# A decoder block on one core: the order of VectorE's work in a Strassen step, and five steps more in Strassen form

## The chip, the core and the metric

The kernel runs on one core of a Trainium2 chip. The metric is the device time of one execution in microseconds, as the median of several runs. The engines are TensorE (PE in the profile, its weight loads PEld), VectorE (DVE), ScalarE (ACT), GpSimd (POOL) and SyncE (SP); transfers run on queues that SP and POOL feed.

## What is computed

The block normalizes a 256x4096 activation, multiplies it with one wide projection, mixes one part by causal averages over four window lengths and one by a gated short convolution, multiplies both with branch weights, merges them by sigmoid gates, multiplies with an output matrix, adds the input, and normalizes again. Cut to what matters:

```
h = rmsnorm(x, norm_w[l])
proj = jnp.einsum('bsd,de->bse', h, w_in[l])              # 4096 x 20480
u_p, z_p, u_c, b_c, c_c, z_c, g_logit = jnp.split(proj, SPLIT_POINTS, axis=-1)
y_pool = causal_multiscale_pool(u_p, pool_w[l], pool_scale[l]) * jax.nn.silu(z_p)
y_conv = causal_gated_shortconv(u_c, b_c, c_c, conv_w[l], conv_b[l]) * jax.nn.silu(z_c)
br = jnp.einsum('bsnc,ncd->bsnd', jnp.stack([y_pool, y_conv], axis=2), w_branch[l])   # 2 x 2048 x 4096
merged = jnp.sum(jax.nn.sigmoid(g_logit.reshape(b, s, 2, d) + gate_b[l]) * br, axis=2)
x = x + jnp.einsum('bsd,de->bse', merged, w_out[l])       # 4096 x 4096
return rmsnorm(x, final_norm_w)
```

All is float32. The kernel writes each factor as a high part, rounded to the format that TensorE multiplies, and a low part, the rest. A product is three matmuls: high by high, high by low, low by high.

## The kernel before

**Units and steps.** The work is a list of units, each 1024 output columns for all 256 rows. In order: cu0, cc0, cz0, cb0 and the same four with 1 (convolution branch), pz0, pu0, pz1, pu1 (pooling branch), eight gate units g0_0, g1_0, g0_1 to g1_3, eight branch units b0_0, b1_0 to b1_3 and four output units o0 to o3. A unit runs over its inner dimension in steps of 256 rows of weights: 16 steps, in a branch unit 8. `SEQUENCES` (L627) has one letter for each step. `p` is a plain step: 2 halves of columns, 2 of inner rows, 2 of tokens and 3 matmuls of 128x512, so 24 matmuls. `s` and `u` are steps in Strassen form: seven products of halves, each of 3 matmuls, so 21. `b` and `m` in two units are the pooling's own matmuls. The rows of cu0 and of the last branch unit, b1_3, are all plain; b0 and b1 stand for all other branch units.

**Preparing a step.** A step's 1 MB of weights lands in one of three `raw` buffers, asked for on SP's queue as soon as the step three places before is split (`pump`, L1199). Then `micros` (L278) writes its high and low parts into pages of `ring`, 16 pages of a 128x512 pair each. For a plain step that is twice: ScalarE rounds 128x1024 (`split_act`, L257), VectorE subtracts (`split_sub`, L261); 4 pages. A Strassen step needs four sums of weight quarters beside three quarters as they are, 7 pages:

- `sums`: VectorE adds the first quarter to the second and third, 128x1024 into `V`. In a *helped* step this isn't done by VectorE: the quarters are loaded into a free corner of `E` or `R` and POOL's queue adds the others on the way. A step with `s` is helped if a corner is free in time; a step with `u` never is.
- `direct`: ScalarE rounds three quarters (128x1536); VectorE adds the third sum into the first quarter of `raw`, subtracts for the three quarters, and adds the fourth sum into the second quarter.
- `t13`: high and low of the first two sums.
- `t24`: high and low of the third and fourth sum, one 128x1024 on ScalarE and one on VectorE.

A page is free again when TensorE has used it, and ScalarE, the first to write, waits for that. Every engine works in the order in which the program issues (`keep_in_program_order`). Steps are prepared up to three (AHEAD) before TensorE's own.

**Multiplying.** A Strassen step's products go to eight banks of sums: four that plain steps use too (`sums`, PE[t][n]), and four more (`shared`). In code: `order = N3, M1, M2, N7, N5, N6, N4`, where N3, M1, M2 use the pages of `direct`, N7, N5 those of `t13`, N6, N4 those of `t24`. The first six matmuls go to a `sums` bank and a shared one, and the tenth, the first of N7, to `shared(2)`. In a unit that ends with a Strassen step that step's order is N3, M2, N4, M1, N7, N5, N6.

**Around a unit's end.** The shared banks are joined by `joins` (L450): on VectorE four to six operations of 128x512 from them into `R`. If the unit's last Strassen step is not its last step, the joins are queued early, one for every six matmuls of the step that follows; else `combine` (L497) issues them behind the last step. Then `R` and `E` are added, and a unit's own epilogue follows by such ticks: for cb0 (`b_epi`, L675) a load of `E`, a multiplication of `R` by `E`, and 16 transposes of `R` on TensorE through the shared banks, whose results VectorE multiplies into `Y`.

Of the kernel before, what the change touches and what calls it, by code (L numbers as in the profile page):

```python
# [59 lines left out]
def hybrid_block(ctx: ExitStack, tc: tile.TileContext, x, x_t, norm_t, w_first, w_in, pool_w, pool_scale,  # L60
# [10 lines left out]
    def act(dst, src, func=AF.Copy, **kw):  # L71
        return pin(nc.scalar.activation(dst, src, func, **kw))  # L72

    def tt(dst, a, b, op):
        return pin(nc.vector.tensor_tensor(out=dst, in0=a, in1=b, op=op))  # L75
# [4 lines left out]
    def add(dst, a, b):  # L80
        return tt(dst, a, b, ALU.add)

    def sub(dst, a, b):
        return tt(dst, a, b, ALU.subtract)
# [161 lines left out]
    def parts_of(block):  # L246

        return [(i, m, ring[:, 4 * KB * pg:4 * KB * (pg + m)].rearrange("p (i a n) -> p i a n", i=m, a=2))
                for i, pg, m in runs(block)]

    def high(pg):
        return ring[:, 4 * KB * pg:4 * KB * pg + NH]

    def low(pg):
        return ring[:, 4 * KB * pg + NH:4 * KB * (pg + 1)]

    def split_act(block, src):  # L257
        for i, m, d in parts_of(block):
            act(d[:, :, 0], src[:, i:i + m])

    def split_sub(block, src):  # L261
        for i, m, d in parts_of(block):
            sub(d[:, :, 1], src[:, i:i + m], d[:, :, 0].bitcast(F32))

    def place_of_sum(i):

        return (E, R)[i // 2][:, i % 2].rearrange("p (i n) -> p i n", i=2)


    class Step:  # L270
# [7 lines left out]
        def micros(self):  # L278

            r = None if self.src is None else self.raw  # L280

            def half(n):
                def f(block):
                    self.blocks[n] = block
                    q = r.rearrange("p (n k c) -> p n k c", n=2, k=2)[:, n]
                    if self is steps[0]:

                        for k in range(2):
                            act(high(block[k]), q[:, k])
                            if n == 0 and k == 0:  # L290
                                x_direct(0)
                            sub(low(block[k]), q[:, k], high(block[k]).bitcast(F32))
                        return
                    split_act(block, q)
                    split_sub(block, q)
                return f

            if self.kind == "P":
                self.blocks = [None] * 2
                return self.pre + [(2, None, half(0)), (2, None, half(1))] + self.post  # L300
            if self.kind == "S":
                q = r.rearrange("p (i n) -> p i n", i=4)

                helped = self.slot is not None
                v = place_of_sum(self.slot) if helped else V

                def sums(_):
                    add(V, q[:, 0:1].to_broadcast([P, 2, NH]), q[:, 1:3])

                def direct(block):  # L310
                    self.bd = block
                    split_act(block, q[:, 1:4])
                    add(q[:, 0], v[:, 0], q[:, 2])
                    split_sub(block, q[:, 1:4])
                    add(q[:, 1], q[:, 0], q[:, 3])

                def t13(block):
                    self.b13 = block
                    split_act(block, v)
                    split_sub(block, v)  # L320
                    self.summed = now[0]

                def t24(block):
                    self.b24 = block
                    split_act(block, q[:, 0:2])
                    split_sub(block, q[:, 0:2])
                    self.split = True

                return self.pre + self.post + ([] if helped else [(0, None, sums)]) + [(3, lambda: not helped or self.added, direct), (2, None, t13), (2, None, t24)]
            if self.kind == "B":  # L330
                def parts(block):
                    self.block = block
                    split_act(block, R.rearrange("p t (n c) -> p (t n) c", c=NH))
                    split_sub(block, R.rearrange("p t (n c) -> p (t n) c", c=NH))

                return [(4, lambda: self.unit.flags.get("base"), parts)]
            if self.kind == "M":
                g = self.g
                e = E[:, g].rearrange("p (o c) -> p o c", o=2)

                def weights(block):
                    self.bw = block
                    q = r.rearrange("p (k n) -> p k n", k=4)
                    split_act(block, q)
                    split_sub(block, q)

                def pooled(block):
                    self.ba = block
                    split_act(block, e)
                    split_sub(block, e)  # L350

                return [(4, None, weights), (2, lambda: self.unit.flags.get(f"pooled{g}"), pooled)]
# [265 lines left out]
    def turned(n, kinds):  # L618

        kinds = [k for k in kinds if k in "psu"]  # L620
        np_ = kinds.count("p")
        ps, ss = iter(range(np_)), iter(range(np_, n))
        return [("P", next(ps)) if k == "p" else (k.upper(), next(ss)) for k in kinds]

    N = NP_X + NS_X
    LAST_FIRST = ("cc0",)
    SEQUENCES = {'cc0': 'ppspspsspspssppp', 'cz0': 'pppppspssspspsss', 'cb0': 'psppspssspspspss', 'cu1': 'ppppspsssspsspss', 'cc1': 'ppsppsssspsspssp', 'cz1': 'pppppssssspsssps', 'cb1': 'pspspspsspsspssp', 'pz0': 'ppppspssssspusps', 'pu0': 'ppsspspsppsspsss', 'pz1': 'ppbpmmpsssspssspsps', 'pu1': 'ppssspppsspsspss', 'g0_0': 'ppbpmmpspspspsssssp', 'g1_0': 'ppppsspssssspssp', 'g0_1': 'ppppssssspspssps', 'g1_1': 'psppsssspsspspps', 'g0_2': 'ppppsssssspssppu', 'g1_2': 'puppsssspspssspp', 'g0_3': 'pppspssussssppsp', 'g1_3': 'pspsppsspspspups', 'b0': 'pppppsps', 'b1': 'pppspsps', 'o0': 'ppppppsspssspspu', 'o1': 'pppssspsppsspsps', 'o2': 'pspsspppsspsusps', 'o3': 'psppsspsspspsppp'}  # L627
    seqs_y = [turned(ny, SEQUENCES[f"b{n}"]) for n in range(2)]
    seq_0 = [("P", i) for i in range(N)]
    seq_yp = [("P", i) for i in range(ny)]  # L630

    def in_unit(name, col, epi, seq=None, **kw):
        def src(i):
            return win[col // NU, i]
        if seq is None:
            seq = turned(N, SEQUENCES[name])
            if name in LAST_FIRST:
# [177 lines left out]
    def out_unit(c):  # L815
# [12 lines left out]
        def src(i):  # L828
            return wout[c, i]
        seq = turned(N, SEQUENCES[f"o{c}"])  # L830
        units.append(Unit(f"o{c}", src, seq, m_ops, epi, before=start))
# [132 lines left out]
    def insert(u, c, owner):  # L964
# [4 lines left out]
        plain = iter(main)  # L969
        for k in SEQUENCES[u.name]:  # L970
            seq.append(next(more[k] if k in more else plain))
# [6 lines left out]
    for c in range(2):  # L978
        i = units.index(with_band[c])
# [85 lines left out]
    def x_direct(p):  # L1065
        o = x_ops[p]
        b = xc(p)
        for part in range(2):
            for k in range(2):
                q = b[:, k].rearrange("p (t c) -> p t c", t=2)  # L1070
                if o.kind == "P":
                    h, l = (o.view[:, a, 1 - k] for a in range(2))
                else:
                    at = (direct_at(p), A12)[k]
                    h, l = (o.view[:, a, at:at + 2] for a in range(2))
                if part == 0 and p == 0 and k == 0:
                    pin(nc.vector.tensor_scalar(out=h, in0=q, scalar1=col(p, k), scalar2=None, op0=ALU.mult))
                elif part == 0:
                    act(h, q, scale=col(p, k))
                else:  # L1080
                    stt(l, q, col(p, k), h.bitcast(F32), ALU.mult, ALU.subtract)
        o.ready = True
# [218 lines left out]
    def order_of(seq):  # L1301
        return [i for _, i in seq]

    def queue_fills():
# [6 lines left out]
        def from_y(n, o, i, ready=None):  # L1311
            later(o, y_d[n, i // 4][:, i % 4].rearrange("p k t -> p (k t)"), place_of(o),
                  ready or (lambda: n == 0 or units_done[0]))
# [14 lines left out]
        for n in DIRECT_LAST:  # L1328
            for i in range(NP_Y[n], ny):
                from_y(n, y_last[n][i], i, lambda: all(o.ready for q in y_ops for o in q))  # L1330
        for i in order_of(turned(N, SEQUENCES["o0"])):
            from_m(m_ops[i], i)
# [247 lines left out]
```

## Time and profile before

| | |
|---|---|
| median of 3 runs | 2366.35 us (2365.9 to 2366.68) |
| the profiled execution | 2366.37 us, span 2364.7 us |
| granted TensorE clock | 0.998 |
| busy | PE 99%, PEld 82%, DVE 95%, ACT 60%, POOL 5% |
| read from HBM | 554.48 MB, 245 GB/s with what is written |

Busy time of PE counts each matmul from its start to its modelled end, and neighbours overlap: a 128x512 matmul lasts 0.39 us in the profile but the next starts sooner, so TensorE's work is read from how far the starts lie apart. In rows of a timeline the first number is the start, the second the time from the start to the end of a merged group, and `x3` the number of instructions merged. Brackets at a row's end name idle time before it and what released it.

### The profile page before, as it was taken

How to read it: one execution, taken by the hardware profiler on the slowest of the kernel's cores; microseconds unless marked ns; L12 is line 12 of the kernel's file. 1: busy time of each engine (PE TensorE's matmuls, PEld its weight loads, DVE VectorE, ACT ScalarE, POOL GpSimd, SP SyncE). 2: the span in 40 equal slices, each digit the busy share in tenths (PEclk: the TensorE clock that was granted, in tenths of full speed). 3: DMA queues.
4: the chain of work that ended last, by engine and by line, in shares of the span. 5: the costliest groups of instructions: out<-in, count | busy, mean ns of one | idle time of the engine just before them, and what ended most of it. 6: DMA issues, size and time to landing. Idle time of an engine off the chain costs nothing.

```text
span 2364.7 us, 29447 instructions
## 1 busy us (share of the span) xinstructions
PE 2348.5 (99%) x10462; PEld 1942.6 (82%) x10462; DVE 2235.7 (95%) x2378; ACT 1427.6 (60%) x1558; POOL 113.0 (5%) x168
## 2 busy tenths in 40 slices
PE   9999999999999999999999999999999999999998
PEld 7888887888888888888888888888888888888886
DVE  8999999999999999999999999999998898899998
ACT  8565665666655666566566656666665556556564
POOL 0000000000011002000000000000000000000000
PEclk9999999999999999999999999999999999999999
DMA  9677777877886768768997888888866768678877
GB/s 346 193 227 224 218 247 245 271 241 215 259 278 197 237 211 260 230 217 265 279 281 239 274 244 265 265 265 275 264 236 234 259 231 307 203 227 277 254 231 271
DMA packets 164515, 588.94 MB, mean 249 GB/s; under 512 B 18448, under 2 KB 18704, under 8 KB 160272
## 3 DMA queue, kind: packets, MB, share of 16 engines
q1 hardware_dynamic: 146128, 510.49, 64.3%
q0 software_dynamic: 17808, 75.51, 13.3%
q8 instruction: 82, 1.34, 0.2%
q10 hardware_dynamic: 432, 1.07, 0.1%
q14 instruction: 65, 0.53, 0.1%
HBM read 554.48 MB, written 25.17 MB: 245 GB/s over the span
## 4 chain that ended last, share of the span: by engine, by line
PE 88%; DVE 7%; issue 2%; ACT 1%; DMA 1%; DVEq 0%; ACTq 0%
PE sums L1282 65%; PE shared L1282 22%; DVE ring L75 4%; DVE raw L75 1%; ACT ring L72 1%; PE shared L764 1%; DVE R L75 1%; DVE V L75 1%; PE shared L546 1%; DMA raw<-in_w_out_dram 0%; DMA raw<-in_w_in_dram 0%; DVE sa L75 0%; PE shared L1012 0%; PE shared L742 0%; DVE Y L87 0%
## 5 line engine op out<-in xcount | busy, mean ns | idle before, releaser
L1282 PE MATMUL sums<-ring,arena 128*128 128x512 f32 x7536 | 1786.5, 390 | 0.6 <-ACT E L72 0.3
L1282 PEld LDWEIGHTS sums<-ring,arena 128*128 128x128 f32 x7536 | 1412.0, 188 | 294.7 <-DVE ring L75 1.8
L72 ACT ACTIVATE ring<-raw 128x1024 fp32r<-128x1024 f32 (+3 forms) x977 | 1011.7, 1083 | 580.6 <-DVE raw L75 366.3
L75 DVE TENSOR_TENSOR ring<-raw,ring 128x1024 fp32r<-128x1024 f32 (+3 forms) x977 | 1195.1, 1258 | 73.3 <-ACT ring L72 59.9
L1282 PE MATMUL shared<-ring,arena 128*128 128x512 f32 x2568 | 648.8, 389 | 1.4 <-DVE R L75 1.2
L1282 PEld LDWEIGHTS shared<-ring,arena 128*128 128x128 f32 x2568 | 481.6, 188 | 103.3 <-DVE R L75 2.6
L72 ACT ACTIVATE ring<-V 128x1024 fp32r<-128x1024 f32 (+1 forms) x165 | 172.1, 1045 | 204.1 <-DVE V L75 171.9
L75 DVE TENSOR_TENSOR V<-raw 128x1024 f32<-128x1024 f32 x162 | 197.7, 1220 | 4.9 <-DMA raw<-in_w_in_dram 4.9
L75 DVE TENSOR_TENSOR ring<-V,ring 128x1024 fp32r<-128x1024 f32 (+1 forms) x165 | 197.8, 1200 | 1.3 <-ACT ring L72 1.3
L75 DVE TENSOR_TENSOR raw<-raw 128x512 f32<-128x512 f32 x214 | 148.0, 691 | 6.3
L75 DVE TENSOR_TENSOR raw<-V,raw 128x512 f32<-128x512 f32 x162 | 112.1, 692 | 4.9
L75 DVE TENSOR_TENSOR R<-R,E 128x1024 f32<-128x1024 f32 (+1 forms) x49 | 77.5, 1591 | 0.9
L75 DVE TENSOR_TENSOR R<-R,shared 128x512 f32<-128x512 f32 x103 | 69.9, 685 | 7.6 <-ACT R L72 5.0
L97 POOL DMA_DIRECT2D E<-in_w_in_dram x34 | 29.6, 872 | 640.2 <-DMA E<-in_w_in_dram 370.7
L72 ACT ACTIVATE arena<-sa 128x512 fp32r<-128x512 f32 (+2 forms) x49 | 25.8, 556 | 53.8 <-DVE sa L75 53.7
L72 ACT ACTIVATE E<-sums,rin 128x512 f32<-128x512 f32 x76 | 48.3, 680 | 13.3 <-PE sums L1282 13.3
L75 DVE TENSOR_TENSOR ring<-E,ring 128x1024 fp32r<-128x1024 f32 (+1 forms) x45 | 52.5, 1171 | 1.9 <-ACT ring L72 1.9
L72 ACT ACTIVATE ring<-E 128x1024 fp32r<-128x1024 f32 (+1 forms) x45 | 45.1, 1006 | 0.2
L75 DVE TENSOR_TENSOR arena<-sa,arena 128x512 fp32r<-128x512 f32 (+2 forms) x49 | 28.2, 601 | 2.1 <-ACT arena L72 2.1
L75 DVE TENSOR_TENSOR raw<-E,raw 128x512 f32<-128x512 f32 x39 | 26.7, 684 | 0.0
L72 ACT ACTIVATE E<-sums 128x512 f32<-128x512 f32 x40 | 22.4, 591 | 5.9 <-PE sums L1282 5.8
L72 ACT ACTIVATE R<-R 128x2048 f32<-128x2048 f32 x8 | 15.4, 1920 | 16.8 <-DVE R L75 16.8
(141 smaller groups left out, 550.1 us busy)
## 6 DMA issues: line engine op xcount, KB each, us to landing
raw<-in_w_in_dram SPq DMA_DIRECT2D x589, 512.0 KB, 4.6
raw<-in_w_branch_dram SPq DMA_DIRECT2D x128, 512.0 KB, 4.9
raw<-in_w_out_dram SPq DMA_DIRECT2D x123, 512.0 KB, 4.6
E<-in_w_in_dram SPq DMA_DIRECT2D x34, 512.0 KB, 6.4
E<-in_w_in_dram POOLq DMA_DIRECT2D x34, 512.0 KB, 8.9
raw<-in_w_in_dram SPq DMA_DIRECT2D x47, 256.0 KB, 3.9
gates_d<-R POOLq DMA_DIRECT2D x8, 1024.0 KB, 10.4
R<-in_w_in_dram SPq DMA_DIRECT2D x13, 512.0 KB, 8.2
```

What stands on the lines that cost most here:

```text
L72: return pin(nc.scalar.activation(dst, src, func, **kw))
L75: return pin(nc.vector.tensor_tensor(out=dst, in0=a, in1=b, op=op))
L97: return pin(nc.gpsimd.dma_start(dst, src, accum_op=ALU.add))
L546: pin(nc.tensor.transpose(shared(j)[:, i * T + t * P:i * T + (t + 1) * P], src[:, t, c:c + P], ident))
L764: pin(nc.tensor.matmul(o, a, b, start=(k, i) == (0, 0), stop=(k, i) == (3, 2)))
L1282: pin(nc.tensor.matmul(ps, lhs, rhs, start=n == 0, stop=n == u.total[b] - 1))
```

## The change

Two edits in `micros` and new sequences. In `direct` the subtraction for the three quarters stands ahead of the third sum, so that the two sums are neighbours. In `t24` ScalarE rounds the third and the fourth sum in an instruction each.

```
                 def direct(block):
                     self.bd = block
                     split_act(block, q[:, 1:4])
+                    split_sub(block, q[:, 1:4])
                     add(q[:, 0], v[:, 0], q[:, 2])
-                    split_sub(block, q[:, 1:4])
                     add(q[:, 1], q[:, 0], q[:, 3])
...
                 def t24(block):
                     self.b24 = block
-                    split_act(block, q[:, 0:2])
+                    for i in range(2):
+                        act(high(block[i]), q[:, i])
                     split_sub(block, q[:, 0:2])
                     self.split = True
```

`SEQUENCES`, the entries that differ (the rest is the same):

```
      before                after
cb0   psppspssspspspss      psppspssspssspsp
cb1   pspspspsspsspssp      ppsssppsspsspssp
pu1   ppssspppsspsspss      ppssspppsspsspus
g1_0  ppppsspssssspssp      pppssspsspssspsp
g0_1  ppppssssspspssps      psppssssusspspsp   one more
g1_1  psppsssspsspspps      psppssuspsssspps   one more
g1_2  puppsssspspssspp      puppsssssspsspsp   one more
g0_3  pppspssussssppsp      pppspssssssspupp
g1_3  pspsppsspspspups      pppsuspssspppuss   one more
o0    ppppppsspssspspu      ppppppssppsssspu
o1    pppssspsppsspsps      pppssspspsssppus   one more
o2    pspsspppsspsusps      pspsspppsspsuups
o3    psppsspsspspsppp      pspspspsspspsppp
```

With the branch units counted as often as they run, the program has 214 Strassen and 234 plain steps before, and 219 and 229 after. Of the 219, by the change's own words, 54 are helped.

More of the change, by code (lines that the diff above doesn't have):

```diff
@@ L312, in direct @@
                     split_act(block, q[:, 1:4])
+                    split_sub(block, q[:, 1:4])
                     add(q[:, 0], v[:, 0], q[:, 2])
-                    split_sub(block, q[:, 1:4])
                     add(q[:, 1], q[:, 0], q[:, 3])
@@ L324, in t24 @@
                     self.b24 = block
-                    split_act(block, q[:, 0:2])
+                    for i in range(2):
+                        act(high(block[i]), q[:, i])
                     split_sub(block, q[:, 0:2])
@@ L626, in hybrid_block @@
     LAST_FIRST = ("cc0",)
-    SEQUENCES = {'cc0': 'ppspspsspspssppp', 'cz0': 'pppppspssspspsss', 'cb0': 'psppspssspspspss', 'cu1': 'ppppspsssspsspss', 'cc1': 'ppsppsssspsspssp', 'cz1': 'pppppssssspsssps', 'cb1': 'pspspspsspsspssp', 'pz0': 'ppppspssssspusps', 'pu0': 'ppsspspsppsspsss', 'pz1': 'ppbpmmpsssspssspsps', 'pu1': 'ppssspppsspsspss', 'g0_0': 'ppbpmmpspspspsssssp', 'g1_0': 'ppppsspssssspssp', 'g0_1': 'ppppssssspspssps', 'g1_1': 'psppsssspsspspps', 'g0_2': 'ppppsssssspssppu', 'g1_2': 'puppsssspspssspp', 'g0_3': 'pppspssussssppsp', 'g1_3': 'pspsppsspspspups', 'b0': 'pppppsps', 'b1': 'pppspsps', 'o0': 'ppppppsspssspspu', 'o1': 'pppssspsppsspsps', 'o2': 'pspsspppsspsusps', 'o3': 'psppsspsspspsppp'}
+    SEQUENCES = {'cc0': 'ppspspsspspssppp', 'cz0': 'pppppspssspspsss', 'cb0': 'psppspssspssspsp', 'cu1': 'ppppspsssspsspss', 'cc1': 'ppsppsssspsspssp', 'cz1': 'pppppssssspsssps', 'cb1': 'ppsssppsspsspssp', 'pz0': 'ppppspssssspusps', 'pu0': 'ppsspspsppsspsss', 'pz1': 'ppbpmmpsssspssspsps', 'pu1': 'ppssspppsspsspus', 'g0_0': 'ppbpmmpspspspsssssp', 'g1_0': 'pppssspsspssspsp', 'g0_1': 'psppssssusspspsp', 'g1_1': 'psppssuspsssspps', 'g0_2': 'ppppsssssspssppu', 'g1_2': 'puppsssssspsspsp', 'g0_3': 'pppspssssssspupp', 'g1_3': 'pppsuspssspppuss', 'b0': 'pppppsps', 'b1': 'pppspsps', 'o0': 'ppppppssppsssspu', 'o1': 'pppssspspsssppus', 'o2': 'pspsspppsspsuups', 'o3': 'pspspspsspspsppp'}
     seqs_y = [turned(ny, SEQUENCES[f"b{n}"]) for n in range(2)]
```

## The prediction

> **What bounds the kernel now.** I read the page first, then the groups of instructions by shape, then a stretch from the middle, and last the timelines of the places where TensorE's starts lie too far apart.
>
> ```profile
> span 2364.7 us, 29447 instructions
> PE 2348.5 (99%) x10462; PEld 1942.6 (82%) x10462; DVE 2235.7 (95%) x2378; ACT 1427.6 (60%) x1558; POOL 113.0 (5%) x168
> ```
>
> ```profile
> L1282 PE MATMUL sums<-ring,arena 128*128 128x512 f32 x7536 | 1786.5, 390 | 0.6 <-ACT E L72 0.3 <-DVE ring L75 0.3
> L1282 PE MATMUL shared<-ring,arena 128*128 128x512 f32 x2568 | 648.8, 389 | 1.4 <-DVE R L75 1.2
> ```
>
> ```profile
> core 0: us, PE busy (x) PEld busy (x) DVE busy (x) ACT busy (x) POOL busy (x), PEclk, DMA share, GB/s
> 1530.00:1590.00 60.00, 60.00 (x267) 49.67 (x266) 58.31 (x55) 36.47 (x34) 2.57 (x3) 1.00 0.85 259
> ```
>
> 267 matmuls touch 60 us, the first having begun up to 0.39 us earlier: one starts every (60 + 0.39) / 267 = 0.2262 us, or 0.2270 if one of them only touches the edge. I use 0.2265. The 10104 matmuls of the two groups then take 2288.5 of 2364.7 us; the rest is the start, the end, transposes, the pooling's matmuls and a few stalls. **TensorE's matmul count is the bound, with VectorE close behind**: in that stretch VectorE is busy 58.31 of 60 us. ScalarE has 40% of the time free. So two questions: how many matmuls go, and does VectorE, which writes what TensorE reads, still keep up?
>
> **What TensorE loses.** Five plain steps of 24 matmuls become Strassen steps of 21. That is 15 matmuls, 15 x 0.2265 = 3.40 us. This term is certain as long as TensorE streams.
>
> **What VectorE pays for a step.** Here are the groups, and one Strassen step that is not helped, from its first sum (351.40) to the instruction behind it (358.09).
>
> ```profile
> L75 DVE TENSOR_TENSOR ring<-raw,ring 128x1024 fp32r<-128x1024 f32 x665 | 788.7, 1222 | 64.8 <-ACT ring L72 51.9
> L72 ACT ACTIVATE ring<-raw 128x1024 fp32r<-128x1024 f32 x665 | 675.9, 1054 | 465.5 <-DVE raw L75 348.8 <-PE sums L1282 67.4 <-PE shared L1282 15.4
> L75 DVE TENSOR_TENSOR ring<-raw,ring 128x1536 fp32r<-128x1536 f32 x184 | 322.4, 1752 | 3.9 <-ACT ring L72 3.6
> L75 DVE TENSOR_TENSOR V<-raw 128x1024 f32<-128x1024 f32 x162 | 197.7, 1220 | 4.9 <-DMA raw<-in_w_in_dram 4.9
> L75 DVE TENSOR_TENSOR raw<-raw 128x512 f32<-128x512 f32 x214 | 148.0, 691 | 6.3
> L75 DVE TENSOR_TENSOR raw<-V,raw 128x512 f32<-128x512 f32 x162 | 112.1, 692 | 4.9
> L72 ACT ACTIVATE ring<-raw 128x512 fp32r<-128x512 f32 x124 | 73.9, 620 | 23.9 <-DVE raw L75 17.5 <-DMA raw<-in_w_in_dram 2.2 <-PE sums L1282 2.1
> L75 DVE TENSOR_TENSOR R<-R,shared 128x512 f32<-128x512 f32 x103 | 69.9, 685 | 7.6 <-ACT R L72 5.0
> ```
>
> ```profile
> 344.16 1.40 DVE L75 TENSOR_TENSOR R<-R,shared 128x512 f32<-128x512 f32 x2
> 345.48 0.68 DVE L75 TENSOR_TENSOR R<-shared,R 128x512 f32<-128x512 f32 x1
> 346.20 0.69 DVE L75 TENSOR_TENSOR R<-R,shared 128x512 f32<-128x512 f32 x1
> 346.92 2.29 DVE L75 TENSOR_TENSOR R<-R,E 128x2048 f32<-128x2048 f32 x1
> 349.13 2.35 DVE L75 TENSOR_TENSOR ring<-raw,ring 128x1024 fp32r<-128x1024 f32 x2
> 351.40 1.22 DVE L75 TENSOR_TENSOR V<-raw 128x1024 f32<-128x1024 f32 x1
> 352.65 0.69 DVE L75 TENSOR_TENSOR raw<-V,raw 128x512 f32<-128x512 f32 x1
> 353.26 1.75 DVE L75 TENSOR_TENSOR ring<-raw,ring 128x1536 fp32r<-128x1536 f32 x1
> 355.05 0.69 DVE L75 TENSOR_TENSOR raw<-raw 128x512 f32<-128x512 f32 x1
> 355.66 1.22 DVE L75 TENSOR_TENSOR ring<-V,ring 128x1024 fp32r<-128x1024 f32 x1
> 356.95 1.23 DVE L75 TENSOR_TENSOR ring<-raw,ring 128x1024 fp32r<-128x1024 f32 x1
> 358.09 2.29 DVE L75 TENSOR_TENSOR R<-R,E 128x2048 f32<-128x2048 f32 x1
> ```
>
> ```profile
> 346.27 1.49 ACT L72 ACTIVATE ring<-raw 128x1536 fp32r<-128x1536 f32 x1 [0.90 <-PE sums L1282]
> 352.74 1.06 ACT L72 ACTIVATE ring<-V 128x1024 fp32r<-128x1024 f32 x1 [4.97 <-DVE V L75]
> 355.86 3.05 ACT L72 ACTIVATE ring<-raw 128x1024 fp32r<-128x1024 f32 x4 [2.06 <-DVE raw L75]
> ```
>
> Look at the joints. The subtraction at 353.26 needs nothing from the sum at 352.65 and starts 0.08 us before that ends (352.65 + 0.69 = 353.34). The sum at 352.65 reads what the instruction before it wrote, and starts 0.03 after its end (352.62); so does the one at 355.05, which overwrites a quarter that the subtraction ahead of it reads. **A dependent neighbour costs 0.117 us** (0.034 + 0.083, with the digits of the group means: a 1.222 us instruction is followed after 1.139). The third price is the wait at the end. The fourth sum ends at 355.74, ScalarE starts to round at 355.86, needs 1.06, and VectorE starts at 356.95, though its instruction before ended at 356.88: 0.07 of gap and 0.08 of lost overlap, 0.157 in all.
>
> In the new order the subtraction stands behind `sums` without needing it, and the third sum behind the subtraction without needing it: two dependent joints go. One comes: the fourth sum now reads its neighbour. And `t24`: ScalarE rounds the third sum while VectorE makes the fourth; behind the fourth it has 0.12 + 0.62 us to go (0.62 from the 128x512 group), while VectorE subtracts `t13` for 1.14. That wait goes. A step that is not helped takes 358.09 - 351.40 = 6.69 before and 6.69 - 0.117 - 0.157 = 6.42 after. A helped one has no `sums` joint to lose: 6.69 - 1.25 = 5.44 before (without the sum and its gap), 5.28 after. A plain one takes 2 x 1.139 = 2.28 in both.
>
> **VectorE's total.** 162 of 214 Strassen steps are not helped, so 52 are; after, 165 and 54. The order gives back 165 x 0.274 + 54 x 0.157 = 53.7 us at most (nothing, if none of the waits goes). Five added steps, of which two more helped, cost 3 x 6.42 + 2 x 5.28 - 5 x 2.28 = 18.4. VectorE gains 35 us on the whole.
>
> **Does it fit where the steps are added?** While TensorE works on a plain step (24 x 0.2265 = 5.44 us), VectorE prepares one in 2.28 and gets 3.16 ahead. On a Strassen step (4.76) it falls back: by 1.93, or 0.68 when helped, on the average of the shares 1.63; after, 1.66 and 0.52, on the average 1.38. A gate unit's end needs six 128x512 operations and two of 1.22, about 4.0 + 2.3 = 6.3 us. So 7 plain and 9 Strassen steps leave 22.1 - 14.6 - 6.3 = +1.2 before and +3.4 after; 6 and 10 leave 19.0 - 13.8 - 6.3 = -1.1 after, and would have left -3.6 at the old price. Three gate units (g0_1, g1_1, g1_2) get ten. They overdraw 3.3 us in all, against +3.4 in each unit of nine around them. The ring's 16 pages cap what is carried over, so I expect some new stall: between 0 and 3.3, and I take 0.8, near the lower end, because the units between refill.
>
> **ScalarE and the transfers.** Two roundings of 0.62 replace one of 1.05: at most 0.19 us x 219 = 42, and some 8 for the added steps, on an engine that is idle 2364.7 - 1427.6 = 937 us. The rounding of the three quarters is asked for one sum earlier. It ended at 347.76 here, 5.5 us before VectorE used it, and that cover is needed (rival below). A step's weights are the same 1 MB in either form; two more helped steps move a few hundred KB more each. I cost both at nothing.
>
> **Where TensorE stalls now, and what becomes of it.**
>
> ```profile
> 266.63 0.84 PE L1282 MATMUL sums<-ring,arena 128*128 128x512 f32 x3
> 267.74 1.43 PE L1282 MATMUL shared<-ring,arena 128*128 128x512 f32 x5 [0.27 <-DVE R L75]
> ...
> 358.31 0.84 PE L1282 MATMUL sums<-ring,arena 128*128 128x512 f32 x3
> 360.44 0.66 PE L546 MATMUL shared<-ident,R 128*128 128x128 f32 x4 [1.29 <-DVE R L75]
> ...
> 596.65 0.84 PE L1282 MATMUL sums<-ring,arena 128*128 128x512 f32 x3
> 598.47 1.20 PE L1282 MATMUL shared<-ring,arena 128*128 128x512 f32 x4 [0.98 <-DVE R L75]
> ...
> 1009.62 2.20 PE L1282 MATMUL sums<-ring,arena 128*128 128x512 f32 x9
> 1012.10 0.73 PE L1282 MATMUL sums<-ring,arena 128*128 128x512 f32 x2 [0.28 <-DVE ring L75]
> ...
> 1113.78 1.29 PE L1282 MATMUL sums<-ring,arena 128*128 128x512 f32 x5
> 1115.36 1.43 PE L1282 MATMUL sums<-ring,arena 128*128 128x512 f32 x5 [0.29 <-ACT E L72]
> ```
>
> A train of n should be followed after n x 0.2265. The five places lose 0.43 (cb0), 1.45 (cu1), 1.14 (cb1), 0.44 (pu1) and 0.45 us (g1_0).
> - cb0: N7 wants `shared(2)`, which cz0's joins still read; VectorE does them late, behind a backlog of Strassen work. Two steps of that backlog at 0.27 less cover 0.43. Gone.
> - cb1: the same, but the first Strassen step moves from the second place to the third, 5.44 us later. Gone.
> - cu1: transposes wait for the multiplication that VectorE starts at 358.09. Its chain from 344.16 has no idle time. cb0 now ends on a plain step, so the four joins (344.16 to 346.89, 2.73 us) run during that step and leave the chain. Gone.
> - pu1: the pages of the last Strassen step come 0.44 late; eight Strassen steps ahead of it are cheaper by 0.16 to 0.27 each, one may lose its help for 1.25. Gone, barely.
> - g1_0: ScalarE empties a bank late, behind roundings that wait for ring pages, that is for TensorE. Nothing there changes. Stays.
>
> 3.46 us go. **The sum**, against the profiled execution's 2366.37 us (1.7 more than its span, and as good as the median of 2366.35): 2366.37 - 3.40 - 3.46 + 0.8 = 2360.3 us.
>
> **The rivals.** *TensorE's saving alone.* The stalls at unit heads are set by banks and by the ring, and wait for other work instead; 2366.4 - 3.4 = 2363.0. For it: only a few of VectorE's waits are on the chain. Against: in four of the five places VectorE is the releaser and works without a break up to the stall. 0.19.
>
> *Reordering frees nothing.* If VectorE paid for every neighbour alike, only the 0.157 of `t24` would be won, a Strassen step would still cost 1.46 of lead, a unit of ten would overdraw 19.0 - 14.6 - 6.3 = -1.9, three of them 5.7. With the two stalls that need no cheaper step gone (1.45 + 1.14): 2366.4 - 3.4 - 2.6 + 5.7 = 2366.1 with no cover, 2363 with half. Against it stand the starts themselves, 0.08 early or 0.03 late by dependence. 0.06. The Trainium skill's page "VectorE: DVE Perf Modes", section "The DRAIN you can't avoid", has such a rule: the next instruction does not start until the pipeline is empty, with or without semaphores between them, so the order of neighbours would not matter. By the rule the time would be this rival's; this trace does not agree with it, since independent neighbours overlap by 0.083 us; the page itself lets an instruction that is not held start earlier.
>
> *Slower: ScalarE has no time in hand.* The subtraction for the three quarters now needs ScalarE's 1.49 us rounding 0.72 us sooner (one sum and its joint). Where ScalarE finishes it just in time today, VectorE waits that long, and a Strassen step is no cheaper: three units of ten overdraw 3 x 3.6 = 10.8, and the time is 2366.4 - 3.4 + 10.8 = 2373.8. It ends above 2371 once a step is cheaper by less than 0.09 us on the average instead of 0.25 (then each overdraws 2.7, 8.1 in all). Likeliest for a helped step right behind another Strassen step, where no `sums` lies between. Against it: the 5.5 us in hand above, and ScalarE idle 4.97 us behind that rounding. 0.05.
>
> **How the numbers follow.** No change can be told from 0.2%, 4.7 us, either way: below 2361.6 is faster. My forecast has 0.70; 0.04 of it lies above that line, with new stalls of over 2.1. Faster 0.66; same 0.04 + 0.19 + 0.06 = 0.29; slower 0.05. The low end takes all five stalls (3.91), none new, and 1.5 for the matmul behind each, late too (1.43 for five where 4 x 0.2265 + 0.39 = 1.30), and for shorter stalls that I don't quote: 2357.2. The high end is the first rival with half of the overdraft: 2363.0 + 1.6 = 2364.6.
>
> **What would show it right or wrong.** In the profile after: 15 matmuls fewer at L1282; the sum into the first quarter starting 0.08 before the end of the 128x1536 subtraction, and the fourth sum 0.03 behind the third; VectorE's last subtraction of a step starting before the one ahead ends, so that the 51.9 us of its 128x1024 group's waits for ScalarE shrink by some 10; no stall at the tenth matmul of the first Strassen step of cb0 and cb1, none at cu1's first transposes. Wrong: the 128x1536 subtraction waiting for ScalarE in many steps, or TensorE waiting for ring pages in g0_1, g1_1 and g1_2 for over 3 us.

## The result and the profile after

The changed kernel takes 2359.82 us (median of 10 runs, 2357.42 to 2362.45) against 2366.51 before (2365.71 to 2368.42) on the same chip: a ratio of 0.9971, interval 0.9962 to 0.9981. It is faster by 6.7 us; the forecast was 2360.3. The profiled execution took 2359.81, its span is 6.6 us shorter than that of before.

The page, and VectorE's and ScalarE's groups by shape:

```profile
span 2358.1 us, 29784 instructions
PE 2343.8 (99%) x10447; PEld 1939.8 (82%) x10447; DVE 2227.8 (94%) x2382; ACT 1477.7 (63%) x1757; POOL 115.5 (5%) x171
```

```profile
L75 DVE TENSOR_TENSOR ring<-raw,ring 128x1024 fp32r<-128x1024 f32 x660 | 781.6, 1220 | 52.9 <-ACT ring L72 52.3
L75 DVE TENSOR_TENSOR ring<-raw,ring 128x1536 fp32r<-128x1536 f32 x195 | 342.0, 1754 | 22.3 <-ACT ring L72 22.1
L72 ACT ACTIVATE ring<-raw 128x512 fp32r<-128x512 f32 x520 | 322.4, 630 | 309.3 <-DVE raw L75 255.0 <-PE sums L1283 23.7 <-PE shared L1283 10.3
L75 DVE TENSOR_TENSOR V<-raw 128x1024 f32<-128x1024 f32 x164 | 199.9, 1219 | 1.9 <-issue 1.3 <-DMA raw<-in_w_in_dram 0.5
L75 DVE TENSOR_TENSOR raw<-V,raw 128x512 f32<-128x512 f32 x164 | 112.4, 685 | 0.0
```

TensorE has 15 instructions fewer (10462 to 10447). VectorE makes 164 first sums, so 55 of 219 Strassen steps are helped, one more than the change's words say. The sum into the first quarter has lost its 4.9 us of idle time ahead (last row). The idle time ahead of the 128x1536 subtraction grew from 3.9 to 22.3 us: it now meets ScalarE.

The step that the prediction took apart, in cu1, on VectorE and with ScalarE's roundings beside it:

```profile
347.99 1.22 DVE L75 TENSOR_TENSOR V<-raw 128x1024 f32<-128x1024 f32 x1
349.12 1.75 DVE L75 TENSOR_TENSOR ring<-raw,ring 128x1536 fp32r<-128x1536 f32 x1
350.79 0.68 DVE L75 TENSOR_TENSOR raw<-V,raw 128x512 f32<-128x512 f32 x1
351.51 0.69 DVE L75 TENSOR_TENSOR raw<-raw 128x512 f32<-128x512 f32 x1
352.12 1.22 DVE L75 TENSOR_TENSOR ring<-V,ring 128x1024 fp32r<-128x1024 f32 x1
353.25 1.22 DVE L75 TENSOR_TENSOR ring<-raw,ring 128x1024 fp32r<-128x1024 f32 x1
354.39 2.28 DVE L75 TENSOR_TENSOR R<-R,E 128x2048 f32<-128x2048 f32 x1
```

```profile
349.32 1.07 ACT L72 ACTIVATE ring<-V 128x1024 fp32r<-128x1024 f32 x1 [2.41 <-DVE V L75]
351.57 2.42 ACT L72 ACTIVATE ring<-raw 128x512 fp32r<-128x512 f32 x4 [1.18 <-PE sums L1283]
```

Only one joint of VectorE is left, 350.79 + 0.68 to 351.51. The last subtraction starts at 353.25, before 352.12 + 1.22 = 353.34: no wait for ScalarE. The step takes 354.39 - 347.99 = 6.40 us, where 6.42 was forecast.

TensorE at the heads of cb0 and cu1, where it lost 0.43 and 1.45 us, and then at the heads of b1_0 and o1, where it lost nothing before:

```profile
266.14 0.84 PE L1283 MATMUL sums<-ring,arena 128*128 128x512 f32 x3
266.82 1.98 PE L1283 MATMUL shared<-ring,arena 128*128 128x512 f32 x8
...
356.77 1.53 PE L1283 MATMUL sums<-ring,arena 128*128 128x512 f32 x6
358.14 0.60 PE L547 MATMUL shared<-ident,R 128*128 128x128 f32 x4
...
1716.14 1.66 PE L1283 MATMUL sums<-ring,arena 128*128 128x512 f32 x6 [0.44 <-ACT E L72]
1718.59 1.64 PE L1283 MATMUL sums<-ring,arena 128*128 128x512 f32 x6 [0.80 <-ACT E L72]
...
2101.23 1.52 PE L1283 MATMUL sums<-ring,arena 128*128 128x512 f32 x6
2103.22 2.12 PE L1283 MATMUL sums<-ring,arena 128*128 128x512 f32 x8 [0.47 <-ACT E L72]
```

At 266.82 and 358.14 a train follows when it should (266.14 + 3 x 0.2265 = 266.82). After 1716.14 the next train should come at 1717.50 and comes 1.09 late; after 2101.23 at 2102.59, and comes 0.63 late. Both wait for ScalarE to empty a bank into `E`. What ScalarE does there:

```profile
1714.56 1.05 ACT L72 ACTIVATE ring<-raw 128x1024 fp32r<-128x1024 f32 x1
1715.51 0.57 ACT L72 ACTIVATE E<-sums 128x512 f32<-128x512 f32 x1
1717.00 1.06 ACT L72 ACTIVATE ring<-raw 128x1024 fp32r<-128x1024 f32 x1 [0.91 <-DMA raw<-in_w_branch_dram]
1717.96 1.07 ACT L72 ACTIVATE E<-sums 128x512 f32<-128x512 f32 x2
...
2099.39 0.58 ACT L72 ACTIVATE E<-sums 128x512 f32<-128x512 f32 x1
2101.62 1.06 ACT L72 ACTIVATE ring<-raw 128x1024 fp32r<-128x1024 f32 x1 [1.65 <-DMA raw<-in_w_out_dram]
2102.59 1.07 ACT L72 ACTIVATE E<-sums 128x512 f32<-128x512 f32 x2
```

Between two emptyings stands the rounding for a step to come, its weights have not landed, and the emptying queues behind it. Weights that land late have taken the place of VectorE's backlog.

For every unit I added up how far TensorE's starts lie apart beyond the pace (0.2266 us behind a 128x512 matmul, 0.113 behind 256 columns, 0.06 behind 128). What is left is lost time, with a constant share for transposes (0.96 in cu1). The last row is the time from the last matmul's start to the span's end. The kernels of the right columns are those of the next section.

| us lost in | before | changed | order only | sequences only | one rounding | all but g1_3 |
|---|---|---|---|---|---|---|
| cb0, cu1, cb1 | 4.78 | 1.20 | 1.18 | 2.36 | 2.48 | 1.32 |
| pu0, pu1, g1_0 | 1.72 | 0.06 | 0.22 | 2.47 | 3.56 | 0.24 |
| g0_1 to g1_3 | 0.60 | 0.57 | 0.12 | 6.78 | 5.40 | 0.57 |
| b0_0, b1_0 | 0.02 | 2.22 | 0.02 | 2.90 | 3.23 | 0.02 |
| o1, o2, o3 | 0.13 | 1.30 | 0.13 | 2.81 | 2.91 | 0.30 |
| whole program | 21.26 | 18.50 | 15.51 | 31.75 | 31.72 | 16.06 |
| behind the last matmul | 12.05 | 11.61 | 10.53 | 13.72 | 12.47 | 10.90 |

So the 6.6 us are 3.4 of matmuls, 21.26 - 18.50 = 2.8 of stalls, and 0.4 at the end. Of the stalls, 5.2 us went in the first two rows and 3.4 came in the branch and output units; 0.9 more went elsewhere, half of it in the first unit.

The sum is firmer than its parts. In a second profile of the changed kernel ("changed again" below) the span is 2358.1 us too, and TensorE loses 18.8 us, but the five rows read 1.79, 0.85, 0.58, 1.13 and 0.50, and the first unit loses 0.8 us more than here. In that execution cb0 (some 50 us behind its head) and g1_0 lose 0.80 us each, more than before the change (0.58 and 0.60).

### The profile page after: what moved, and what is told of

Same layout as the page of the kernel before. It is cut to its first block, busy times and chain, and to the rows that moved or that the text cites. A ratio compares the mean times of both kernels' runs of the same rounds, so it can differ in the third digit from the quotient of the medians.

```text
span 2358.1 us, 29784 instructions
## 1 busy us (share of the span) xinstructions
PE 2343.8 (99%) x10447; PEld 1939.8 (82%) x10447; DVE 2227.8 (94%) x2382; ACT 1477.7 (63%) x1757; POOL 115.5 (5%) x171
## 3 DMA queue, kind: packets, MB, share of 16 engines
q10 hardware_dynamic: 432, 1.07, 0.1%
## 4 chain that ended last, share of the span: by engine, by line
PE 92%; DVE 5%; DMA 1%; issue 1%; ACT 1%; DVEq 0%; ACTq 0%
PE sums L1283 67%; PE shared L1283 23%; DVE ring L75 3%; DMA raw<-in_w_out_dram 1%; PE shared L765 1%; DVE raw L75 1%; PE shared L547 1%; DVE R L75 1%; DVE V L75 0%; ACT ring L72 0%; DMA raw<-in_w_branch_dram 0%; PE shared L1013 0%; ACT E L72 0%; PE shared L743 0%; PE shared L744 0%
## 5 line engine op out<-in xcount | busy, mean ns | idle before, releaser
L1283 PEld LDWEIGHTS sums<-ring,arena 128*128 128x128 f32 x7452 | 1395.9, 188 | 292.4 <-ACT E L72 3.4
L72 ACT ACTIVATE ring<-raw 128x1024 fp32r<-128x1024 f32 (+2 forms) x1172 | 1055.8, 939 | 482.5 <-DVE raw L75 255.0
L75 DVE TENSOR_TENSOR ring<-raw,ring 128x1024 fp32r<-128x1024 f32 (+2 forms) x965 | 1192.5, 1274 | 77.1 <-ACT ring L72 76.3
L72 ACT ACTIVATE ring<-R 128x1024 fp32r<-128x1024 f32 (+1 forms) x16 | 18.4, 1153 | 12.1 <-DVE R L75 11.7
```

The source lines that it names most:

```text
L1283: pin(nc.tensor.matmul(ps, lhs, rhs, start=n == 0, stop=n == u.total[b] - 1))
```

## The experiments

Medians, ranges, and the ratio to the kernel before on the same chip, with its interval:

| kernel | matmuls | us (range) | ratio |
|---|---|---|---|
| order only | as before | 2359.5 (2359.15 to 2359.8) | 0.9966 (0.9954 to 0.9979) |
| sequences only | -15 | 2374.21 (2373.27 to 2375.13) | 1.0028 (1.0017 to 1.0040) |
| changed, one rounding | -15 | 2375.02 (2373.88 to 2376.45) | 1.0032 (1.0019 to 1.0045) |
| changed, old order of VectorE | -15 | 2360.13 (2358.2 to 2362.09) | 0.9966 (0.9953 to 0.9978) |
| order, three gates | -9 | 2359.78 (2358.56 to 2360.52) | 0.9967 (0.9955 to 0.9980) |
| order, g1_3 | -3 | 2362.4 (2360.33 to 2363.29) | 0.9980 (0.9971 to 0.9988) |
| order, output units | -3 | 2358.86 (2358.64 to 2360.12) | 0.9966 (0.9954 to 0.9978) |
| changed again | -15 | 2359.78 (2357.37 to 2361.02) | 0.9967 (0.9954 to 0.9979) |
| order, gates and output | -12 | 2357.63 (2357.13 to 2358.88) | 0.9956 (0.9944 to 0.9969) |
| two roundings only | as before | 2360.12 (2359.61 to 2360.69) | 0.9966 (0.9952 to 0.9979) |
| neighbours only | as before | 2367.33 (2365.15 to 2368.11) | 0.9997 (0.9988 to 1.0006) |
| changed, all but g1_3 | -12 | 2357.91 (2357.31 to 2358.2) | 0.9956 (0.9943 to 0.9968) |

The first four, the next four and the last four ran on three chips, where the kernel before took 2367.76, 2366.94 and 2366.90 us. Between these groups the ratios can be compared, while a difference of less than 1 us between times can come from the chip.

And what a Strassen step that follows another one costs VectorE in them, as the median distance between their last subtractions where nothing else lies between:

| us | not helped | helped |
|---|---|---|
| before; sequences only | 6.69 | 5.43 |
| changed; order only | 6.40 | 5.27 |
| two roundings, old order of VectorE | 6.53 | 5.27 |
| one rounding, new order of VectorE | 6.57 | 5.67 |

**Order only.** The changed kernel with `SEQUENCES` as before.

> Both edits of the step's order, with the sequences of before: 214 Strassen steps, no matmul less. Theory A (TensorE's count is the bound, cheaper Strassen steps only take stalls away that come from VectorE's backlog): the stalls of cb0 (0.43 us), pu1 (0.44) and g1_2 (0.22) go, those that a place in the sequence makes, cu1 (1.45) and cb1 (1.14), get shorter by the backlog saved, some 1 to 2 us together; 2363.0 to 2365.0, VectorE's busy time lower by 1 to 2 us only, because what goes is lost overlap and idle time. Theory B (the order frees nothing that counts): 2366.4, all five stalls in place. Theory C (VectorE itself is the bound): 214 steps cheaper by 0.25 us each give 2366.4 - 53 = 2313 us at most, and at least 2350.

Measured 2359.5: the whole gain, with not a matmul less. The span of its profile is 7.3 us shorter than before: 5.7 of stalls, and 1.5 behind the last matmul, where VectorE now has time to wait 0.82 us for TensorE and before worked without a pause. Theory A named the mechanism and missed its size; its 2363 to 2365 is wrong, B and C are too. The groups, and the head of cb1 on TensorE:

```profile
L75 DVE TENSOR_TENSOR ring<-raw,ring 128x1024 fp32r<-128x1024 f32 x665 | 787.5, 1219 | 53.2 <-ACT ring L72 51.7
L75 DVE TENSOR_TENSOR ring<-raw,ring 128x1536 fp32r<-128x1536 f32 x184 | 322.5, 1753 | 26.1 <-ACT ring L72 25.8
```

```profile
593.85 0.84 PE L1283 MATMUL sums<-ring,arena 128*128 128x512 f32 x3
594.58 1.65 PE L1283 MATMUL shared<-ring,arena 128*128 128x512 f32 x6
```

The tenth matmul of cb1's first Strassen step, still in the second place of the unit, follows 0.05 late, where it was 1.14 (the unit loses 0.20 in all). cu1 loses only its transposes' share. In this execution neither stall needs another sequence. VectorE's waits for ScalarE did not shrink by the 10 us that I named (51.7 and 25.8 us; before, 51.9 and 3.6). VectorE is ahead more often and waits for free pages by way of ScalarE, whose own waits for matmuls of the first four banks rose from 121.4 to 154.7 us in the list of waits. In the changed kernel VectorE's waits did not shrink either (52.3 us for the 128x1024 group), though that wait of ScalarE's is 121.9 there; so the reason holds at most for this kernel.

**Sequences only.** The kernel before with the new `SEQUENCES`.

> The new sequences with the old order inside a Strassen step. Theory A: 15 matmuls less (-3.4 us), the stalls of cu1 and cb1 gone by their places (-2.6), but a gate unit of ten Strassen steps overdraws VectorE's lead by 3.6 us, three of them by up to 10.8, and TensorE waits for ring pages in g0_1, g1_1, g1_2: 2363 to 2371, my value 2367. Theory B: the same as the changed kernel, 2359.8, the sequences do it all.

Measured 2374.2, slower than before by 0.28% (0.17% to 0.40%), and above my range. The gate units lose 6.78 us, 3.7 of them in the three that could overdraw 10.8 at most, and the branch and output units 5.6 more than before, which I had not counted. But cu1 loses 0.96 us, its transposes' share, and cb1 0.02: the new sequences take these two stalls away without a cheaper step. In g1_2 TensorE waits for ring pages:

```profile
1478.16 1.07 PE L1282 MATMUL sums<-ring,arena 128*128 128x512 f32 x4
1479.61 0.73 PE L1282 MATMUL sums<-ring,arena 128*128 128x512 f32 x2 [0.38 <-DVE ring L75]
```

The changed kernel has no such wait in a gate unit. This is the case for the order: without it the new sequences lose.

**One rounding.** The changed kernel with the rounding of `t24` undone:

```
                 def t24(block):
-                    for i in range(2):
-                        act(high(block[i]), q[:, i])
+                    split_act(block, q[:, 0:2])
```

> The changed kernel, but the third and fourth sum rounded in one instruction again. Theory A: VectorE waits for ScalarE behind t13 again, 0.157 us in most of 219 steps, 1.6 us in a unit of ten; that overdraws g0_1, g1_1 and g1_2 by 2.7 us each at most, and some of it shows as stalls: 2360 to 2364, my value 2361.5. Theory B (the wait was hidden anyway): 2359.8.

Measured 2375.0, 15 us above the changed kernel and far out of my range. I had priced only the wait of `t24`. VectorE first in this kernel, for two helped steps in a row of g1_2, with ScalarE's roundings beside it, then VectorE for the same two steps in the changed one:

```profile
1480.30 1.22 DVE L75 TENSOR_TENSOR ring<-E,ring 128x1024 fp32r<-128x1024 f32 x1
1481.59 3.13 DVE L75 TENSOR_TENSOR ring<-raw,ring 128x1024 fp32r<-128x1024 f32 x2
1484.64 0.69 DVE L75 TENSOR_TENSOR raw<-E,raw 128x512 f32<-128x512 f32 x1
...
1480.50 2.44 ACT L72 ACTIVATE ring<-raw 128x1024 fp32r<-128x1024 f32 x2 [2.29 <-DVE raw L75]
```

```profile
1471.02 1.22 DVE L75 TENSOR_TENSOR ring<-E,ring 128x1024 fp32r<-128x1024 f32 x1
1472.15 2.89 DVE L75 TENSOR_TENSOR ring<-raw,ring 128x1024 fp32r<-128x1024 f32 x2
1474.96 0.68 DVE L75 TENSOR_TENSOR raw<-E,raw 128x512 f32<-128x512 f32 x1
```

The two merged instructions are `t24`'s subtraction and the next step's over three quarters. They take 3.13 us instead of 2.89: with the single rounding ScalarE is done with the three quarters, the second of its merged pair, only at 1480.50 + 2.44 = 1482.94, and VectorE, which now asks for them first, could have started some 0.2 us sooner, at 1481.59 + 1.14 = 1482.73. This is the slower rival of the prediction, in the helped steps where I expected it; the second rounding is what keeps it away.

**Old order of VectorE.** The changed kernel, with `add(q[:, 0], ...)` ahead of `split_sub` in `direct` again.

> The changed kernel, but the third sum ahead of the subtraction for the three quarters again; the two roundings stay apart. Theory A: a step that is not helped loses 0.117 us for the dependent joint behind its first sum, a helped one nothing; a unit of ten overdraws 1.9 us instead of 1.1: 2359.5 to 2362.5, my value 2360.5, so less than the single rounding costs. Theory B (a neighbour costs the same whether it depends or not): 2359.8, and starts that lie 0.08 us before the end of the instruction in front everywhere.

Measured 2360.1, within the range and not to be told from the changed kernel. The dependent joint costs what the trace said (6.53 against 6.40 us), but 0.13 us in such a step does not show in the time.

**Three gates, g1_3, output units, and the changed kernel again.** Both edits of the order and the old sequences, but for the units named.

> Both edits of the step's order, the sequences of before, but the new ones of g1_0, g0_1, g1_1, g1_2 and g0_3: three of the five added Strassen steps (9 matmuls less). The order alone gave 2359.5. Theory D (an added step saves its 0.68 us unless it makes ScalarE wait for weights with the emptying of a bank queued behind, as in b0_0, b1_0 and o1 of the changed kernel): no such place is touched here, so 2359.5 - 2.0 = 2357.5, no stall over 0.3 us in the gate units. Rival E (VectorE's lead is spent, added steps come back as waits for ring pages in the gate units): 2359.5.

> Both edits, the sequences of before, but the new one of g1_3: one added Strassen step. Theory D: 0.68 us less in matmuls, and the stalls at the head of b0_0 and b1_0 that the changed kernel has (0.3 and 1.8 us) come with it: 2359.5 - 0.7 + 2.1 = 2360.9. Rival E: 2358.8, no stall there, since neighbouring units keep the old load.

> Both edits, the sequences of before, but the new ones of o0 to o3: one added Strassen step. Theory D: 0.68 us less, and the stalls at the head of o1 (0.74) and o2 (0.36) come with it: 2359.5 - 0.7 + 1.1 = 2359.9. Rival E: 2358.8.

> The changed kernel once more, on the chip of these three, so that they can be set against it: 2359 to 2361 by its own runs. With theory D it stands between the kernel with three added steps in the gates (faster) and the one with g1_3 alone (slower).

g1_3 alone costs 2362.4 - 2359.5 = 2.9 us, or 0.14% by the ratios (3.3 us), though it saves 0.7: theory D's direction, with a larger price. Its fastest run, 2360.33, is slower than the slowest of "order only", 2359.8. ScalarE and TensorE at the head of b1_0 in that kernel:

```profile
1711.81 1.05 ACT L72 ACTIVATE arena<-sa 128x512 fp32r<-128x512 f32 x2 [3.38 <-DVE sa L75]
1712.76 3.04 ACT L72 ACTIVATE ring<-raw 128x512 fp32r<-128x512 f32 x4
...
1717.26 0.59 ACT L72 ACTIVATE E<-sums 128x512 f32<-128x512 f32 x1
...
1718.69 0.58 ACT L72 ACTIVATE E<-sums 128x512 f32<-128x512 f32 x1
```

```profile
1715.94 2.88 PE L1283 MATMUL shared<-ring,arena 128*128 128x512 f32 x12
1719.33 2.86 PE L1283 MATMUL sums<-ring,arena 128*128 128x512 f32 x11 [0.50 <-ACT E L72]
```

By the kernel's code the last unit over the input frees the places of its operands in the order of its steps, and the fills of the next operands (`arena<-sa`) follow. Such a fill stands here ahead of the emptyings, while in "order only" two of them stand behind (at 1717.92, after emptyings at 1714.08 and 1715.53). ScalarE waits 3.38 us for VectorE's sums for it, everything behind it slips, the emptyings of banks at 1717.26 and 1718.69 among it, and TensorE, released by the second, stands 0.67 us at 1719.33. So here the emptying queues behind a fill; late weights are the other cause, not the only one.

The output units give 2358.86 us, the rival's number. But the ratio is that of "order only", 0.9966, so a saving of 0.64 us can't be told from none. The new sequences alone do not bring the changed kernel's stalls: o1 to o3 lose 0.17 us in this profile. Still, the profiles with them and two roundings lose between 0.17 and 1.30 us there ("gates and output", without g1_3's step, 1.05), those with the old ones and two roundings between 0.13 and 0.27. What decides among them is open. The changed kernel again takes 2359.8, as before and as the three gates do, so it does not lie between those and g1_3 as theory D wanted.

The three gates give 2359.8, where theory D wanted 2357.5. In its profiled execution (2359.95) no start in g0_1 to g1_3 is more than 0.02 us late, so the rival's reason, waits for ring pages there, isn't it either; but it loses 2.03 in cu1 where "order only" loses 0.96, in code that both have in common. ScalarE at the end of cb0, in "order only" and then in this kernel:

```profile
336.56 0.69 ACT L72 ACTIVATE E<-sums,rin 128x512 f32<-128x512 f32 x1 [0.25 <-PE sums L1283]
337.14 1.05 ACT L72 ACTIVATE ring<-raw 128x1024 fp32r<-128x1024 f32 x1
338.09 1.26 ACT L72 ACTIVATE E<-sums,rin 128x512 f32<-128x512 f32 x2
```

```profile
336.76 0.69 ACT L72 ACTIVATE E<-sums,rin 128x512 f32<-128x512 f32 x1 [0.25 <-PE sums L1283]
338.61 1.06 ACT L72 ACTIVATE ring<-raw 128x1024 fp32r<-128x1024 f32 x1 [1.16 <-DMA raw<-in_w_in_dram]
339.58 1.25 ACT L72 ACTIVATE E<-sums,rin 128x512 f32<-128x512 f32 x2
```

The same weights land in time in one execution and 1.16 us late in the other; the joins, the multiplication and cu1's transposes all follow from there. They were asked for 1.18 us later (at 333.89 against 332.71 us) and took 4.64 us instead of 4.27. SyncE asks when VectorE's subtraction has freed the buffer, and VectorE is 1.17 us behind here (its first sum at 320.90 against 319.73). It lost 0.56 us of that at one transfer, asked for at 295.50, which took 8.62 us (7.28 in "order only", asked for at 294.88): ScalarE waited 2.00 us for it instead of 0.66. So a late transfer makes the next requests late too, and a unit's end hangs on it; why that transfer took longer is open.

**Gates and output; two roundings only; neighbours only; all but g1_3.** The first and the last leave out g1_3's added step (the last is the changed kernel with that one entry as before); the two others have the old sequences and one edit of the order each.

> Both edits, the sequences of before, but the new ones of g1_0 to g0_3 and of o0 to o3: four of the five added Strassen steps, all but that of g1_3. If the added steps keep their matmuls' worth (theory D): 2359.5 - 4 x 0.68 = 2356.8. If what three gates alone gave holds (2359.8, nothing) and the output units add their own (2358.9 - 2359.5 = -0.6): 2359.2. My value 2358.3; over 2361 would say that the steps disturb each other.

> The sequences of before, the order of VectorE of before; the third and fourth sum are rounded in two instructions, nothing else. Theory F (of the two edits the rounding alone takes the time; it gives a helped step 5.27 us on VectorE instead of 5.43, another 6.53 instead of 6.69): 2359.5 to 2361, nearly what both edits give, my value 2360.0. Rival G (both edits are needed, each half of it): 2363.

> The sequences of before; VectorE's order is the new one, the third and fourth sum are rounded in one instruction as before. Theory F: a step that is not helped takes 6.57 instead of 6.69 us, but a helped one 5.67 instead of 5.43, because its subtraction for three quarters then waits for ScalarE; 162 x 0.12 gained against 52 x 0.24 lost: 2364 to 2369, my value 2366, so no gain from this edit by itself. Rival G: 2363.

> The changed kernel with the old sequence of g1_3: three matmuls more. Theory D: the stalls at the head of b0_0 and b1_0 (2.2 us in the changed kernel's profile) go for 0.68 us: 2359.8 - 1.5 = 2358.3, or 2357 if g1_3 costs what it did by itself (2362.4 against 2359.5). Rival E (what ends there begins elsewhere): 2360.5.

Theory F holds. Two roundings alone give 2360.1, within 0.6 us of both edits and with the same ratio; the new neighbours alone give 2367.3 against 2366.9, nothing. The profiles agree: with two roundings alone TensorE loses 16.0 us and 10.5 behind the last matmul, close to "order only"; with the neighbours alone 22.1 and 11.6, close to before. The first makes every Strassen step cheaper by 0.16 us; the second makes a step that is not helped cheaper by 0.12 and a helped one dearer by 0.24.

Without g1_3's step the other four are worth something: 2357.6 and 2357.9, where two roundings alone take 2360.1 on the same chip; every run of the two is faster than that kernel's fastest, and their 12 matmuls are 2.7 us. The two differ only in the sequences of cb0, cb1 and pu1, which so are worth nothing here. Both beat the kernel before by 0.44% and the changed kernel's median by some 2 us; the five runs of the last lie between 2357.31 and 2358.20, the 15 of the changed kernel between 2357.37 and 2362.45. The ratios' intervals overlap with the changed kernel's, so 2 us is what the medians say and no more. Where the cost sits is plainer: b0_0 and b1_0 lose 1.1 to 3.2 us in all six profiles with g1_3's new sequence, and 0.02 in all eight without it. That is theory D.

## Why the prediction was right, point by point

- **15 matmuls, 3.40 us**: right, with one pace throughout.
- **What a step costs VectorE**: right to 0.02 us, 6.42 and 5.28 forecast, 6.40 and 5.27 measured. The saving is 0.29 and 0.16 us; 35 us of it on the whole were not on the path, as the bound said: TensorE was busy all along.
- **The stalls of the five places go**: in the first profile they did, g1_0's too, which I had left standing; with the smaller ones in the same units 5.2 us went instead of 3.46. For g1_0 that is luck of the execution: it loses 0.80 us in the second profile. I had read its stall as roundings that wait for ring pages. In the profile before, the rounding right ahead of the emptying (1113.68 us) waits 0.45 us for weights, which is the whole stall; in the second profile two roundings there wait 0.50 and 0.18. So the late weights were to be seen before the change.
- **cu1 and cb1**: I gave their 2.59 us to the new sequences (cb0's end, the third place in cb1). These do take both stalls away ("sequences only"), but the cheaper step does it too ("order only"), so I booked to one edit what either gives, and the two do not add. With two roundings and the old sequences six profiles lose 0.96 to 2.03 us in cu1, 0.02 to 0.78 in cb1 and 0.02 in cb0; with two roundings and the new ones, four profiles lose 0.96 to 1.15, 0.02, and 0.22 to 0.80. In cu1 the new sequence is a second cover: the list of waits has weights 2.0 us late at cb0's end in the changed kernel, 1.5 before, and cu1 loses nothing beyond its transposes after, while "three gates", with cb0's old sequence and weights 1.16 late, loses 1.07.
- **New stalls of 0.8 us in the units of ten Strassen steps**: wrong in place and in size. The gate units lose 0.57, no more than before, and none of it is a stall: no start there is more than 0.02 us late, and 0.15 in each unit of ten is spread over many matmuls, two thirds of it over the 15 that read the operand place `more`. 3.4 us came at the heads of b0_0, b1_0, o1 and o2 (1.5 in the second profile), where ScalarE empties banks behind a rounding whose weights are late, or behind a fill. I had costed ScalarE and the transfers at nothing on the strength of their idle time; an engine that is idle 37% of the time still makes TensorE wait when one of its instructions waits for something else.
- **The sum**: 2360.3 against 2359.8. That it is so close is luck, because the errors nearly cancel: 1.8 + 0.9 us more of stalls gone and 0.4 at the end, 2.6 more come. The added steps as a whole gave nothing: "order only" is as fast as the changed kernel. The low end of the range adds up to 2366.37 - 3.40 - 3.91 - 1.5 = 2357.6, not 2357.2; the result lies inside either way.
- **The signs**: the joints, the 15 matmuls, and the heads of cb0, cb1 and cu1 came as named. VectorE's waits for ScalarE in its 128x1024 group did not shrink by 10 us; they went from 51.9 to 52.3.
- **The rivals**: "TensorE's saving alone" is out, since the stalls went with the saving taken away. "Reordering frees nothing" has the wrong mechanism: the joint is real in the trace (350.79 starts early, 351.51 late). The Trainium skill's page "VectorE: DVE Perf Modes", section "The DRAIN you can't avoid", has the rule that this rival follows, and an exception to it: a next instruction that is not held starts earlier. The trace agrees with the exception, by 0.08 us between independent neighbours. But in the time it was nearly right, as only the wait of `t24` counts; made into a kernel ("old order of VectorE") it gives 2360.1 and not 2363 to 2366, so my price for an overdrawn lead was too high there. "ScalarE has no time in hand" showed itself in the helped steps of the kernels with one rounding.

## What to carry to other kernels

Where TensorE streams, look for the few stalls at the seams and ask which engine's backlog feeds each; here a fraction of a microsecond less in every preparation step removed nearly all that came from VectorE's backlog, and no matmul had to go. Split an instruction of the helper engine where its consumer waits for it, and do it before asking for that engine's results earlier: without the split the reordering gained nothing with either set of sequences (2367.3 against 2366.9 us, 2375.0 against 2374.2). Before adding work to a kernel in balance, see which in-order queue holds the emptying of banks, and what else waits in it.

## What the runs showed of the hardware

A VectorE instruction that depends on its neighbour starts 0.03 us behind its end, an independent one 0.08 us before it. From a sum's end to ScalarE's start took 0.12 us, and from ScalarE's end back to VectorE 0.03 (355.74 to 355.86, 356.92 to 356.95 before). The changed kernel's 15 runs spread over 5 us, the five each of the two kernels without g1_3's step over 0.9 and 1.8, with matmul counts that differ by three. As far as single profiles show it, what differs between executions is when weights land at the ends of units: one transfer took 8.62 us in one execution and 7.28 in another, and the requests behind it went out later too. Why a transfer takes longer was not found.
